# 64-row products of two heads issued alternately into two PSUM banks, and the projections cut into eighths and paced by TensorE time

## The chip, the cores and the metric

One core of one Trainium2 chip runs the program. The time is the device time of that core in microseconds (us). The engines are named as the profile names them: PE is TensorE (PEld its weight loads), DVE is VectorE, ACT is ScalarE, POOL is GpSimd, SP issues the DMAs.

## What is computed

The reference is a trunk of two layers for 1024 latent tokens and 128 context tokens, 1024 wide. Layer 0 (a pooling mixer beside a linear recurrence, then an MLP) is not touched here. In layer 1 one input projection feeds two mixers: a bidirectional RWKV-7 scan with 8 heads of 64, and a bidirectional mLSTM with 4 heads of 128. Their outputs go through one output projection, and an MLP follows.

```python
def step(S, inp):                        # RWKV-7, for each token
    r_t, w_t, k_t, v_t, kk_t, a_t = inp
    sa = jnp.einsum('bhvk,bhk->bhv', S, -kk_t)
    S = (S * w_t[:, :, None, :] + sa[..., None] * (kk_t * a_t)[:, :, None, :]
         + v_t[..., None] * k_t[:, :, None, :])
    y = jnp.einsum('bhvk,bhk->bhv', S, r_t)
    return S, y
...
def odd_mixer(h, P, j, S0, C0, n0, m0):
    z = h @ P['od_w_in'][j]
    zr, zm = jnp.split(z, [RW_COLS], axis=-1)
    y_r, S = rwkv7_mixer(zr, P, j, S0)
    y_m, (C, n, m) = mlstm_mixer(zm, P, j, C0, n0, m0)
    y = jnp.concatenate([y_r, y_m], axis=-1).astype(h.dtype) @ P['od_w_out'][j]
    return y, (S, C, n, m)
```

## The kernel before

The 1152 tokens lie in three blocks of 384 columns (tb). A weight of the large products is split into a high and a low part, so that one 128x128 piece of weight takes three TensorE instructions of 384 columns (L234, L235, L236, function `gemm`). A tile of the input projection (`project`) is 3 blocks of 8 pieces, 24 instructions each.

The change lies in `odd_layer_mixer`, the mixers of layer 1. The RWKV scan is cut into 36 steps: 4 pairs of heads by 9 blocks of 128 tokens. Each block holds four chunks of 64 tokens (u = 0..3, two for each direction), and the two heads of a pair (hh = 0, 1) lie in partitions 0 to 63 and 64 to 127 (`HR`). A step has two parts:

- `prep(n, p, i)`, which does not depend on the scan: loads, the products of the 64-token chunks (tile GB, L1163, 64 rows deep, four for each head), a triangular inverse in fp16 (L1198), and at its end the effect of a chunk on the state (tile EF, L1272, again 64 rows deep, four for each head). For each head the four products fill one PSUM bank, DVE reads it (L1167 and L1168, or L1273), and the next head uses the bank of the same tag again. Two preps are under way at a time, with bank sm0 or sm1 each (`bank = n % 2`).
- `chain_block(p, i)`, the scan itself: two sub-blocks q, the second of which needs the state that DVE makes from the first (L1308). q = 0 uses bank sm2, q = 1 bank sm3. The outputs are read by ACT (L1319) or DVE (L1321).

Beside the scan the main loop of `odd_layer_mixer` emits work from the list `fills`: first `input_pieces`, the rest of the input projection with what follows each tile (`expand`, `gate_part`), and after that `mlstm`. All of these are Python generators: each `yield` ends a piece, and the loop takes pieces from them in turn. In each turn of the loop the chain goes two pieces on, each active prep one, and `fill()` is called 0.29 times (input pieces) or 1.45 times (mLSTM) on average (`R1`, `R2`). A piece of projection is one whole block, 24 TensorE instructions (`GS = 1`). When the list is empty, nothing else is emitted beside the scan.

What the loop emits is the priority, not yet the order: a scheduler orders the instructions of each engine when the program is built. The engines then run their own instructions in that order, and semaphores join them. An fp32 product is one instruction of the program and two records of the trace (so 288 products at L1163 stand as 576); fp16 products and the 384-column ones of `gemm` are one record each.

Of the kernel before, what the change touches and what calls it, by code (L numbers as in the profile page):

```python
# [22 lines left out]
P = 128  # L23
# [25 lines left out]
    pass  # L49

PARAMS = [
    ("c", 8), ("c_ctx", 8), ("norm1_w", 16), ("norm2_w", 16), ("final_norm_w", 8), ("b_mod", 96), ("pool_scale", 4),
# [9 lines left out]
def trunk_kernel(ctx: ExitStack, tc: tile.TileContext, A, outs, dbg=None, upto=99, odd="rm"):  # L64

    nc = tc.nc
# [2 lines left out]
    G.mm, G.wide = 0, True  # L69
    G.split = nc.vector  # L70
    G.odd, G.banks, G.turn = odd, [0, 1, 2, 3], 0
    ve, sc, gp, te, sy = nc.vector, nc.scalar, nc.gpsimd, nc.tensor, nc.sync
# [179 lines left out]
    class Rms:  # L252


        def __init__(self, x):
            self.x, self.acc = x, {}
# [464 lines left out]
    CH = 64  # L721
    DECAY = math.exp(-0.5)
    NCH = NT // P
    HR = [slice(0, 64), slice(64, 128)]
# [3 lines left out]
    def odd_layer_mixer(h, early):  # L728
# [13 lines left out]
        op = es.enter_context(tc.tile_pool(name="op", bufs=1))  # L742
# [6 lines left out]
        Rw = rwkv(zd, zbg, zar, zbk, wend, y, op, fp)  # L749
# [7 lines left out]
        def input_pieces():  # L757
            tiles = [St.tile_g()]
            ml = [St.proj_ml(i) for i in range(16)]
            for p in (1, 2, 3):  # L760
                tiles += [St.proj_rw(p, i) for i in (1, 2, 0)]
                if p == 2:
                    tiles += [St.gates(), -1]
                tiles += [p] + ml[:NML]
                ml = ml[NML:]
            tiles += ml
            side = [(0, St.expand(0))]
            for t in tiles:
                if isinstance(t, int):
                    side.append((t, St.expand(t) if t >= 0 else gate_part()))  # L770
                    continue
                for _ in t:
                    yield
                    if side and not advance(side[0][1]):
# [12 lines left out]
        steps = [(p, i) for p in range(4) for i in range(NCH)]  # L787
# [2 lines left out]
        done = [False] * len(steps)  # L790
        started = [-1, False]

        def fill():

            while fills:
                try:
                    next(fills[0])
                    return
                except StopIteration:
                    fills.pop(0)  # L800
                    if not started[1] and not fills:
                        started[1] = True
                        s1.close()
                        fills.append(mlstm(zm, gates.R, yh, es))

        def advance(g, n=1):
            for _ in range(n):
                try:
                    next(g)
                except StopIteration:  # L810
                    return False
            return True

        while started[0] < 0:
            fill()
        active = {0: preps[0]}
        half = 0
        nstep = len(steps)
        chain, nchain, ready, nxt = None, 0, set(), 1
        quota, urgent = 0.0, []  # L820
        STAG = 11
        R1, R2 = 0.29, 1.45
        while nchain < nstep:
            if chain is None and nchain in ready:
                chain = Rw.chain_block(*steps[nchain])
            if chain is not None and not advance(chain, 2):
                chain = None
                if steps[nchain][1] >= NCH // 2:
                    urgent.append(Rw.finish(*steps[nchain]))
                nchain += 1  # L830
            for n in sorted(active):
                if not advance(active[n]):
                    del active[n]
                    ready.add(n)
            half += 1
            if nxt < nstep and len(active) < 2 and nxt - nchain < NB and (not active or half >= STAG):
                while started[0] < steps[nxt][0]:
                    fill()
                active[nxt] = preps[nxt]
                nxt += 1  # L840
                half = 0
            if urgent and not advance(urgent[0]):
                urgent.pop(0)
            quota += R2 if started[1] else R1
            while quota >= 1.0:
                fill()
                quota -= 1.0
        while fills or urgent:
            if urgent and not advance(urgent[0]):
                urgent.pop(0)  # L850
# [225 lines left out]
    def rwkv(zd, zbg, zar, zbk, wend, y, mp, fp):  # L1076
# [58 lines left out]
        def prep(n, p, i):  # L1135
# [20 lines left out]
            yield  # L1156

            GB = mp.tile([P, 4, 3, CH], F32, tag="GB", name="GB", bufs=2)
            for hh, hr in enumerate(HR):
                pg = smps(bank)  # L1160
                right = cols(AG, hh, PRODUCTS)
                for u in range(4):
                    te.matmul(pg[:, u * P : u * P + P], BK[hr, u], right[hr, u], start=True, stop=True)  # L1163
                pgv = pg.rearrange("p (d c n) -> p d c n", d=2, c=2)
# [103 lines left out]
            for hh, hr in enumerate(HR):  # L1268
                pf = smps(bank)
                right = cols(GB, hh, EFFECT)  # L1270
                for u in range(4):
# [12 lines left out]
        def chain_block(p, i):  # L1284
# [82 lines left out]
        return R_  # L1367

    NB = 3
    GS = 1  # L1370

    class HeadNorm:

# [545 lines left out]
```

## Time and profile before

| | |
|---|---|
| median of 3 runs | 3546.11 us (3545.06 to 3550.35) |
| the profiled execution | 3545.23 us, span of the trace 3543.4 us |
| busy over the span | PE 93%, DVE 57%, ACT 39%, POOL 24% |
| mean granted TensorE clock | 0.947 of 2.4 GHz |
| first products of the scan's step 1 | 1377 us |
| last products of the scan | 2600 us |
| mLSTM, first and last products | 2317 to 2521 us |

The clock column of the profile is the mean of two levels: 1.0 is 2.4 GHz, 0.5 is 1.2 GHz. A mean of 0.95 over a stretch therefore says that a tenth of it ran at the lower one. A busy TensorE counts a product until its result is out; products that follow one another overlap in it.

### The profile page before, as it was taken

Reading aid. Unit: us, or ns where it says so; the run is one execution under the profiler, and the core shown is the slowest. Engines: PE = TensorE matmul, PEld = TensorE weight load, DVE = VectorE, ACT = ScalarE, POOL = GpSimd, SP = SyncE. Lnnn points to the kernel's source line nnn. Section 1 sums busy time; section 2 is a strip of 40 time slices with the busy share of each in tenths; the row PEclk is TensorE's granted clock in tenths of the full one; section 3 lists DMA queues with packets and bytes.
Section 4 is the critical chain, followed back from the end, with each engine's and each line's share of the span. In section 5 each row is a group of like instructions: output and inputs, shape, how many; then the busy total and the mean of one; then the engine's idle time right before and its main releaser. Section 6 shows DMA issues by size and latency. Waiting matters only on the chain. (4 is left out here: it accounts for less than half of the span.)

```text
span 3543.4 us, 54607 instructions
## 1 busy us (share of the span) xinstructions
PE 3312.5 (93%) x21376; PEld 3034.2 (86%) x21376; DVE 2002.5 (57%) x4070; ACT 1385.9 (39%) x2919; POOL 847.5 (24%) x706
## 2 busy tenths in 40 slices
PE   7877999999999987999989899988889999999998
PEld 4766999999999985777777688887679999999998
DVE  6786665555533375677777865567546333333335
ACT  4534332111122254655645565587435122221112
POOL 2232321111111233141232421133013111111112
PEclk9998999999999998988989899999579999999999
DMA  5334312222211124342243422365241111111111
GB/s 207 104 128 159 133 59 85 96 90 90 78 42 42 64 93 123 106 109 80 79 106 97 112 73 71 92 189 150 69 132 64 48 42 42 42 42 42 42 42 72
DMA packets 239971, 313.15 MB, mean 88 GB/s; under 512 B 57362, under 2 KB 183394, under 8 KB 238178
## 3 DMA queue, kind: packets, MB, share of 16 engines
q1 hardware_dynamic: 239714, 309.67, 28.2%
q8 instruction: 168, 2.75, 0.3%
q14 instruction: 89, 0.73, 0.1%
HBM read 250.85 MB, written 58.74 MB: 87 GB/s over the span
## 5 line engine op out<-in xcount | busy, mean ns | idle before, releaser
L234 PE MATMUL mm<-h,w 128*128 128x384 f32 x2552 | 897.6, 352 | 2.3 <-ACT h L503 1.2
L235 PE MATMUL mm<-h,w 128*128 128x384 f32 x2552 | 893.4, 350 | 3.6 <-DVE h L506 1.4
L236 PE MATMUL mm<-h,w 128*128 128x384 f32 x2552 | 891.1, 349 | 2.0 <-POOL w L217 2.0
L217 POOL TENSOR_TENSOR w<-w 128x1024 fp32r<-128x1024 f32 x153 | 371.9, 2431 | 1458.1 <-ACT w L216 1453.6
L216 ACT CAST w<-w 128x1024 fp32r<-128x1024 f32 x211 | 221.1, 1049 | 901.1 <-PE mm L235 779.6
L354 DVE SCALAR_TENSOR_TENSOR x<-mm,mod,x 128x384 f32<-128x384 f32 (+1 forms) x576 | 282.7, 513 | 446.1 <-PE mm L236 419.0
L234 PE MATMUL mm<-uH,w 128*128 128x384 f32 x1536 | 520.0, 339 | 0.0
L236 PE MATMUL mm<-uH,w 128*128 128x384 f32 x1536 | 518.7, 338 | 0.0
L235 PE MATMUL mm<-uL,w 128*128 128x384 f32 x1536 | 518.7, 338 | 0.0
L234 PEld LDWEIGHTS mm<-h,w 128*128 128x128 f32 x2552 | 490.5, 192 | 22.3 <-issue 12.3
L235 PEld LDWEIGHTS mm<-h,w 128*128 128x128 f32 x2552 | 490.9, 192 | 14.8 <-POOL h L506 4.3
L236 PEld LDWEIGHTS mm<-h,w 128*128 128x128 f32 x2552 | 490.7, 192 | 12.2 <-issue 5.3
L374 DVE SCALAR_TENSOR_TENSOR s<-mm,r 128x384 f32<-128x384 f32 x192 | 106.6, 556 | 406.2 <-ACT r L372 406.0
L234 PEld LDWEIGHTS mm<-uH,w 128*128 128x128 f32 x1536 | 288.5, 188 | 2.5 <-issue 2.5
L235 PEld LDWEIGHTS mm<-uL,w 128*128 128x128 f32 x1536 | 288.5, 188 | 0.0
L236 PEld LDWEIGHTS mm<-uH,w 128*128 128x128 f32 x1536 | 288.4, 188 | 0.0
L1111 ACT COPY DB<-YQ 64x256 f16<-64x256 f16 x360 | 144.9, 402 | 152.3 <-DVE YQ L1220 120.0
L372 ACT ACTIVATE r<-mm 128x384 f32<-128x384 f32 x192 | 93.5, 488 | 277.4 <-PE mm L236 276.7
L217 DVE TENSOR_TENSOR uL<-s,uH 128x384 fp32r<-128x384 f32 x192 | 150.2, 782 | 87.6 <-ACT uH L216 87.2
L1220 DVE CAST_PREDICATED YQ<-lm,sm 128x512 f16<-128x512 uint16 x180 | 123.6, 686 | 104.4 <-PE sm L1198 70.4
L1198 PEld LDWEIGHTS <-DB 128*128 128x128 f16 x1728 | 93.6, 104 | 90.0 <-issue 50.3
L216 ACT CAST uH<-s 128x384 fp32r<-128x384 f32 x192 | 98.5, 513 | 143.2 <-DVE s L374 143.1
(374 smaller groups left out, 5121.9 us busy)
## 6 DMA issues: line engine op xcount, KB each, us to landing
w<-in_mlp_w_dram SPq DMA_DIRECT2D x128, 512.0 KB, 3.4
wmod<-in_w_mod_dram SPq DMA_DIRECT2D x80, 512.0 KB, 3.8
w<-in_od_w_in_dram SPq DMA_DIRECT2D x31, 512.0 KB, 3.7
w<-in_od_w_out_dram SPq DMA_DIRECT2D x24, 512.0 KB, 4.0
AG<-zar SPq DMA_DIRECT2D x144, 64.0 KB, 2.3
BK<-zbk SPq DMA_DIRECT2D x72, 128.0 KB, 2.3
hbig<-zm SPq DMA_DIRECT2D x18, 512.0 KB, 4.1
rb<-rowd SPq DMA_DIRECT2D x36, 256.0 KB, 3.7
```

The lines of the kernel that those rows point to most:

```text
L216: sc.copy(Hout, src)
L217: eng.tensor_tensor(Lout, src, Hout.bitcast(F32), op=OP.subtract)
L234: te.matmul(ps, wH[:, k, cols], aH, start=start and k == 0, stop=False)
L235: te.matmul(ps, wH[:, k, cols], aL, start=False, stop=False)
L236: te.matmul(ps, wL[:, k, cols], aH, start=False, stop=stop and k == nk - 1)
L354: ve.scalar_tensor_tensor(xs, ps[:, o], modcol(l, 2 if which == 1 else 5, m, s), xs, op0=OP.mult, op1=OP.add)
L372: sc.activation(r, ps[:, :TB], AF.Relu)
L374: ve.scalar_tensor_tensor(s, ps[:, :TB], 0.0, r, op0=OP.max, op1=OP.mult)
L1111: sc.copy(dst[hr, :, hr], src(hr))
L1198: te.matmul(o[r_, u], lt[r_, u], rt[r_] if rt is i16 else rt[r_, u], start=True, stop=True)
L1220: ve.copy_predicated(YQ.rearrange("p w (d c) n -> p (w d) c n", d=2), lmask(l, 0, 4), pyq.rearrange("p (w c) n -> p w c n", c=2),)
```

## The change

Four things change, all in layer 1's mixers or in how they are emitted.

- `prep`: at both places with 64-row products, the loop over heads and chunks is turned around, so that chunk 0 of head 0 is followed by chunk 0 of head 1 and so on. Head 0 writes the prep's own bank, head 1 bank sm3. DVE reads head 1's bank first. The number of products is the same.
- `chain_block`: both sub-blocks q now write halves of one bank, sm2.
- A projection is emitted in eighths (`GS = 8`): one piece of weight, three TensorE instructions, for each `yield`; `expand` still goes on once for eight of these.
- The loop no longer counts calls of `fill()`. TensorE instructions go through `Counted`, which adds up an assumed time for each (0.175 for a 384-column product of `gemm`, 0.213 for a 128-column fp32 product). `topup(us)` raises a debt and calls `fill()` until the time emitted has reached it: 0.515 in each turn, and half of that after each prep. The chain's two pieces of a turn are put apart, one before the preps and one after.

```diff
+    def matmul(self, out, left, right, **kw):
+        n = math.prod(right.shape[1:])
+        if left.dtype == F16:
+            self.us += max(0.028, n / 2400)
+        elif left.dtype == F32R:
+            self.us += n / 2400 + 0.015
+        else:
+            self.us += 2 * max(n, left.shape[-1] / 1.0) / 1200
+        return self.eng.matmul(out, left, right, **kw)
...
+        def topup(us):
+
+            given[1] += us
+            while fills and given[0] < given[1]:
+                fill()
...
-            if chain is not None and not advance(chain, 2):
+            if chain is not None and not advance(chain, 1):
...
+            topup(DUE)
             for n in sorted(active):
                 if not advance(active[n]):
                     del active[n]
                     ready.add(n)
+                topup(DUE / 2 if active else 0)
...
-            quota += R2 if started[1] else R1
-            while quota >= 1.0:
-                fill()
-                quota -= 1.0
...
-            for hh, hr in enumerate(HR):
-                pf = smps(bank)
-                right = cols(GB, hh, EFFECT)
-                for u in range(4):
-                    te.matmul(pf[:, u * P : u * P + P], WT[hr, u], right[hr, u], start=True, stop=True)
-                ve.tensor_tensor(B.EF[:, hh], pf.rearrange("p (u n) -> p u n", u=4), cols(AG, hh, EFFECT), op=OP.add)
+            rights = [cols(GB, hh, EFFECT) for hh in range(2)]
+            pfs = [smps(bank), smps(3)]
+            for u in range(4):
+                for hh, hr in enumerate(HR):
+                    te.matmul(pfs[hh][:, u * P : u * P + P], WT[hr, u], rights[hh][hr, u], start=True, stop=True)
+            for hh in (1, 0):
+                pf = pfs[hh].rearrange("p (u n) -> p u n", u=4)
+                ve.tensor_tensor(B.EF[:, hh], pf, cols(AG, hh, EFFECT), op=OP.add)
                 yield
...
+            pcs = smps(2).rearrange("p (q d h v) -> p q d h v", q=2, d=2, h=2)
             for q in range(2):
                 us = (1, 2) if q else (0, 3)
-                pc_ = smps(2 + q)[:, : 4 * CH].rearrange("p (d h v) -> p d h v", d=2, h=2)
+                pc_ = pcs[:, q]
...
-    GS = 1
+    GS = 8
```

The order on TensorE at the end of the scan's last step, before (sm is a PSUM bank with the number of its use, GB, WT and EF are tiles of `prep`, XV the state; both uses at L1272 are of the same bank):

```order
L1263 MATMUL sm_26071<-AT_26062,PD_10442 128x128 x4
L1272 MATMUL sm_26079<-GB_25661,WT_26076 128x128 x4
L1272 MATMUL sm_26085<-GB_25661,WT_26076 128x128 x4
L1296 MATMUL sm_26091<-XV_25632,EF_26078 128x64 x4
L1296 MATMUL sm_26100<-XV_25632,EF_26078 128x64 x4
```

The same place in the changed program, where all products stand at a line of `Counted`:

```order
L66 MATMUL sm_26036<-AT_26027,PD_10442 128x128 x4
L66 MATMUL sm_26044<-GB_25390,WT_26041 128x128
L66 MATMUL sm_26045<-GB_25390,WT_26041 128x128
L66 MATMUL sm_26044<-GB_25390,WT_26041 128x128
L66 MATMUL sm_26045<-GB_25390,WT_26041 128x128
L66 MATMUL sm_26044<-GB_25390,WT_26041 128x128
L66 MATMUL sm_26045<-GB_25390,WT_26041 128x128
L66 MATMUL sm_26044<-GB_25390,WT_26041 128x128
L66 MATMUL sm_26045<-GB_25390,WT_26041 128x128
L66 MATMUL sm_26056<-XV_25341,EF_26043 128x64 x8
```

The two heads alternate one by one, each with its own bank. The next rows are the first products (BK, AG) of a step in the middle of the changed program, where the scheduler has placed two of head 0 ahead of two of head 1, with a product of the chain between them:

```order
L66 MATMUL sm_13892<-AG_10447,BK_13866 128x128 x2
L66 MATMUL sm_13844<-XV_13032,EF_13671 128x64 x4
L66 MATMUL sm_13893<-AG_10447,BK_13866 128x128 x2
L66 MATMUL sm_13892<-AG_10447,BK_13866 128x128
L66 MATMUL sm_13893<-AG_10447,BK_13866 128x128
L66 MATMUL sm_13892<-AG_10447,BK_13866 128x128
L66 MATMUL sm_13893<-AG_10447,BK_13866 128x128
```

Here two pairs alternate out of a possible four. Counted over the whole program, 89 pairs of 144 stand next to each other at the first place and 129 of 144 at the second, 218 together; before, it was 1.

The last rows show TensorE while the scan's last step but one ends, before (`mm<-h,w` would be a projection, `hbig` is a tile of the mLSTM):

```order
L1296 MATMUL sm<-XV,EF 128x64 x4
L1198 LDWEIGHTS DB
L1198 MATMUL sm<-YQ,DB 128x64
L1198 LDWEIGHTS DB
L1198 MATMUL sm<-YQ,DB 128x64
```

and at the same place in the changed program:

```order
L66 MATMUL sm<-XV,EF 128x64 x4
L66 LDWEIGHTS DB
L66 MATMUL sm<-YQ,DB 128x64
L66 LDWEIGHTS DB
L66 MATMUL sm<-YQ,DB 128x64
L66 LDWEIGHTS DB
L66 MATMUL sm<-YQ,DB 128x64
L66 LDWEIGHTS DB
L66 MATMUL sm<-YQ,DB 128x64
L70 MATMUL mm<-ident,hbig 128x128 x6
L66 MATMUL mm<-h,w 128x384
L70 MATMUL mm<-ident,hbig 128x128
```

The mLSTM now reaches to the end of the scan: from its last product to the scan's last product TensorE has 357 products before and 77 in the changed program. It begins in both at the same step, the 30th of 36. The number of places at which TensorE turns to a group of 64-row products of `prep` falls from 205 to 144.

## Rows read from the trace of the kernel before

**Rows 1.** The profile's page: the span, and the granted clock in 40 slices.
```profile
span 3543.4 us, 54607 instructions
...
PEclk9998999999999998988989899999579999999999
```

**Rows 2.** Busy time by stretch, layer 1's mixers: stretch, length, engines, clock, DMA.
```profile
core 0: us, PE busy (x) PEld busy (x) DVE busy (x) ACT busy (x) POOL busy (x), PEclk, DMA share, GB/s
...
1377.00:1637.00 260.00, 223.83 (x1605) 180.15 (x1604) 172.31 (x364) 140.07 (x325) 72.39 (x85) 0.84 0.39 105
1637.00:1979.00 342.00, 317.22 (x2570) 262.01 (x2569) 257.29 (x651) 198.52 (x479) 103.40 (x119) 0.94 0.35 94
1979.00:2304.00 325.00, 309.67 (x2666) 261.25 (x2664) 201.13 (x492) 184.26 (x457) 69.08 (x76) 0.94 0.29 85
2304.00:2460.00 156.00, 136.46 (x1292) 123.86 (x1291) 112.11 (x280) 123.22 (x376) 53.05 (x64) 0.98 0.66 183
2460.00:2613.00 153.00, 125.51 (x862) 102.71 (x863) 91.56 (x316) 75.15 (x199) 21.66 (x33) 0.63 0.25 75
2613.00:2700.00 87.00, 87.00 (x502) 86.88 (x500) 47.17 (x75) 36.60 (x54) 23.55 (x18) 1.00 0.40 135
```

**Rows 3.** The same view for three single steps of the scan.
```profile
2136.00:2161.00 25.00, 24.25 (x222) 20.97 (x222) 14.24 (x22) 13.79 (x35) 3.96 (x3) 1.00 0.21 68
...
2004.00:2027.00 23.00, 17.95 (x138) 14.54 (x139) 17.15 (x32) 13.65 (x34) 7.41 (x9) 0.65 0.41 125
1597.00:1637.00 40.00, 39.55 (x297) 32.50 (x296) 25.45 (x70) 21.24 (x51) 7.90 (x8) 0.70 0.22 71
```

**Rows 4.** Groups by line, 1377 to 2613 us: busy, mean ns, idle before.
```profile
L1163 PE MATMUL sm<-AG,BK 64*128 64x128 f32 x576 | 109.4, 320 | 10.1 <-DMA AG<-zar 7.3 <-issue 1.8 <-DVE AG L1168 1.0
...
L1272 PE MATMUL sm<-GB,WT 64*128 64x128 f32 x576 | 92.1, 302 | 7.6 <-DVE EF L1273 5.3 <-ACT WT L1265 2.2
...
L1168 DVE TENSOR_TENSOR AG<-sm,gm 64x512 f32<-64x512 f32 x72 | 49.6, 688 | 2.1
L1273 DVE TENSOR_TENSOR EF<-sm,AG 128x512 f32<-128x512 f32 x72 | 49.5, 688 | 64.2 <-PE sm L1272 61.2 <-DMA AG<-zar 2.7
```

**Rows 5.** TensorE in order of time, near 1900 us: start, length, operation.
```profile
1899.96 0.48 PE L1163 MATMUL sm<-AG,BK 64*128 64x128 f32 x2
...
1903.06 0.34 PE L235 MATMUL mm<-h,w 128*128 128x384 f32 x1
1903.33 1.16 PE L1163 MATMUL sm<-AG,BK 64*128 64x128 f32 x8
1904.41 0.44 PE L236 MATMUL mm<-h,w 128*128 128x384 f32 x1
1904.69 0.34 PE L234 MATMUL mm<-h,w 128*128 128x384 f32 x1
```

**Rows 6.** TensorE in order of time, two 64-row products of `expand`.
```profile
1915.48 0.91 PE L981 MATMUL ex<-wa,lw 64*128 64x384 f32 x2
...
1918.47 0.59 PE L982 MATMUL ex<-wa,lw 64*128 64x384 f32 x1
1918.48 0.59 PE L981 MATMUL ex<-wa,lw 64*128 64x384 f32 x1
1918.90 0.48 PE L982 MATMUL ex<-wa,lw 64*128 64x384 f32 x1
1918.91 0.48 PE L981 MATMUL ex<-wa,lw 64*128 64x384 f32 x1
```

**Rows 7.** Busy time by stretch, the scan's last three steps.
```profile
2460.00:2509.00 49.00, 42.14 (x342) 35.75 (x342) 37.08 (x138) 31.89 (x92) 12.42 (x19) 0.77 0.20 57
2509.00:2544.00 35.00, 32.39 (x181) 24.88 (x179) 17.53 (x57) 15.11 (x39) 2.78 (x4) 0.60 0.31 96
2544.00:2600.00 56.00, 43.55 (x318) 35.32 (x318) 29.55 (x97) 23.36 (x61) 5.55 (x8) 0.56 0.16 51
```

**Rows 8.** TensorE at the end of the last step.
```profile
2590.35 2.07 PE L1272 MATMUL sm<-GB,WT 64*128 64x128 f32 x8 [0.68 <-ACT WT L1265]
2593.21 2.07 PE L1272 MATMUL sm<-GB,WT 64*128 64x128 f32 x8 [0.79 <-DVE EF L1273]
```

**Rows 9.** The readers of the chain's outputs: count, shortest, median and longest ns.
```profile
L1319 ACT COPY ys<-sm x72: 258/260/262, 1458.7 to 2598.6; 64x128 f32<-64x128 f32 x72
...
L1321 DVE TENSOR_TENSOR ys<-ys,sm x72: 272/282/292, 1588.9 to 2600.8; 64x128 f32<-64x128 f32 x72
```

More of the change, by code (lines that the diff above doesn't have):

```diff
@@ L49, with __init__, transpose @@
     pass
+class Counted:
+    def __init__(self, eng):
+        self.eng, self.us = eng, 0.0
+    def matmul(self, out, left, right, **kw):
[7 more added lines that the diff above has]
+        return self.eng.matmul(out, left, right, **kw)
+    def transpose(self, *a):
+        self.us += 0.109
+        return self.eng.transpose(*a)
 PARAMS = [
@@ L71, in trunk_kernel @@
     G.odd, G.banks, G.turn = odd, [0, 1, 2, 3], 0
-    ve, sc, gp, te, sy = nc.vector, nc.scalar, nc.gpsimd, nc.tensor, nc.sync
+    ve, sc, gp, te, sy = nc.vector, nc.scalar, nc.gpsimd, Counted(nc.tensor), nc.sync
     cpool = ctx.enter_context(tc.tile_pool(name="cpool", bufs=1))
@@ L767, in input_pieces @@
             side = [(0, St.expand(0))]
+            n = 0
             for t in tiles:
@@ L773, in input_pieces @@
                     yield
-                    if side and not advance(side[0][1]):
+                    n += 1
+                    if side and n % GS == 0 and not advance(side[0][1]):
                         started[0] = max(started[0], side.pop(0)[0])
@@ L791, in odd_layer_mixer @@
         started = [-1, False]
+        given = [0.0, 0.0]
         def fill():
+            us = te.us
             while fills:
@@ L797, in fill @@
                     next(fills[0])
-                    return
+                    break
                 except StopIteration:
@@ L804, in fill @@
                         fills.append(mlstm(zm, gates.R, yh, es))
+            given[0] += te.us - us
+        def topup(us):
+            given[1] += us
+            while fills and given[0] < given[1]:
+                fill()
         def advance(g, n=1):
@@ L815, in odd_layer_mixer @@
             fill()
+        given[1] = given[0]
         active = {0: preps[0]}
@@ L819, in odd_layer_mixer @@
         chain, nchain, ready, nxt = None, 0, set(), 1
-        quota, urgent = 0.0, []
+        urgent = []
         STAG = 11
-        R1, R2 = 0.29, 1.45
+        DUE = 0.515
         while nchain < nstep:
@@ L834, in odd_layer_mixer @@
                     ready.add(n)
+                topup(DUE / 2 if active else 0)
+            if chain is not None and not advance(chain, 1):
+                chain = None
+                if steps[nchain][1] >= NCH // 2:
+                    urgent.append(Rw.finish(*steps[nchain]))
+                nchain += 1
             half += 1
@@ L1158, in prep @@
             GB = mp.tile([P, 4, 3, CH], F32, tag="GB", name="GB", bufs=2)
-            for hh, hr in enumerate(HR):
-                pg = smps(bank)
-                right = cols(AG, hh, PRODUCTS)
-                for u in range(4):
-                    te.matmul(pg[:, u * P : u * P + P], BK[hr, u], right[hr, u], start=True, stop=True)
-                pgv = pg.rearrange("p (d c n) -> p d c n", d=2, c=2)
+            rights = [cols(AG, hh, PRODUCTS) for hh in range(2)]
+            pgs = [smps(bank), smps(3)]
+            for u in range(4):
+                for hh, hr in enumerate(HR):
+                    te.matmul(pgs[hh][:, u * P : u * P + P], BK[hr, u], rights[hh][hr, u], start=True, stop=True)
+            for hh, hr in reversed(list(enumerate(HR))):
+                right = rights[hh]
+                pgv = pgs[hh].rearrange("p (d c n) -> p d c n", d=2, c=2)
                 gmb = gm[:, hh].unsqueeze(2).to_broadcast([P, 2, 2, P])
@@ L1267, in prep @@
             B.EF = mp.tile([P, 2, 4, P], F32, tag="EF", name="EF", bufs=2)
-            for hh, hr in enumerate(HR):
-                pf = smps(bank)
-                right = cols(GB, hh, EFFECT)
-                for u in range(4):
-                    te.matmul(pf[:, u * P : u * P + P], WT[hr, u], right[hr, u], start=True, stop=True)
-                ve.tensor_tensor(B.EF[:, hh], pf.rearrange("p (u n) -> p u n", u=4), cols(AG, hh, EFFECT), op=OP.add)
+            rights = [cols(GB, hh, EFFECT) for hh in range(2)]
+            pfs = [smps(bank), smps(3)]
+            for u in range(4):
+                for hh, hr in enumerate(HR):
+                    te.matmul(pfs[hh][:, u * P : u * P + P], WT[hr, u], rights[hh][hr, u], start=True, stop=True)
+            for hh in (1, 0):
+                pf = pfs[hh].rearrange("p (u n) -> p u n", u=4)
+                ve.tensor_tensor(B.EF[:, hh], pf, cols(AG, hh, EFFECT), op=OP.add)
                 yield
```

## The prediction

> **What bounds the kernel now.** I first read the page [rows 1]. The clock row shows where to look: from slice 5 on it stands at nine tenths or more, until the mixers of layer 1 begin; there it moves up and down, and it falls to 5 tenths near 2500 us. The change touches nothing else, so only the 1223 us from 1377 to 2600 count; before and after them the sum takes no change.
>
> Next, busy time by stretch [rows 2]. TensorE is busy 86% to 95% of each stretch up to 2304 us, DVE 62% to 75%, ACT 54% to 58%. A busy TensorE could still be one that waits for small products to drain, so the reader should look at one quiet step [rows 3]: from 2136 to 2161 us TensorE is busy 24.25 of 25 us, at full clock, while DVE and ACT are busy for 14 us each. Nobody but TensorE fills that step. A step's length follows TensorE's work: the step at 2004 us has no projection beside it and still takes 23 us, because its clock is 0.65. So in this stage a microsecond of TensorE work that is taken out is mostly a microsecond of time, and a microsecond at the lower clock costs half a microsecond of work.
>
> How much time is spent at the lower clock follows from the mean: a stretch at clock c was there for 2(1-c) of its length. For the first three stretches of [rows 2] that is 0.32 x 260 + 0.12 x 342 + 0.12 x 325 = 163 us; for the last three steps [rows 7] 0.46 x 49 + 0.80 x 35 + 0.88 x 56 = 100 us. The last two of these have little but the scan beside them, since the mLSTM's last product is at 2521 us.
>
> **Part 1: the alternating heads.** 288 products of each kind stand as 576 records [rows 4]. A group of two records takes 0.48 us and one of eight 1.16 us [rows 5], so a record costs (1.16 - 0.48) / 6 = 0.113 us and a product 0.227 us. Whether two products in different halves of the array run side by side can be read from `expand`, whose two products have 64 rows each, in different halves, into different banks [rows 6]: L981 alone takes 0.91 us for its two records; a little later L982 and L981 start 0.01 us apart, twice, and both are done at 1919.39, in 0.92 us. Two cost what one cost. So each pair that stands together in the new order saves one product. The order has 218 such pairs of 288 possible: 218 x 0.227 = 49 us. The lower bound is nothing, if TensorE only waits in the time that it gains; the upper one is 59 us, since about a fifth of the stage runs at the lower clock, where eight records take 2.07 us instead of 1.16 [rows 8]. I take three quarters, **37 us**: in the busiest stretch DVE has a quarter of its time left, and some of what is gained will turn into waiting for it.
>
> A second gain comes with it. A change from `gemm` to 64-row products and back costs TensorE time: in [rows 5] the start of L235 is 0.27 us ahead of the group's first record, and after the group L236 is 0.28 us ahead of L234, where an undisturbed run, the last row of [rows 2], has 87 / 502 = 0.173 us. That is 0.10 us each way. The order has 61 fewer such groups, so 61 x 0.20 = **12 us**; it is between 0 and that if the neighbours were of the same kind. I take it whole.
>
> The Trainium skill, page "TensorEngine Tiling (Array Packing)", section Performance Considerations, speaks against this part: tiling speeds up TensorE and not the reading of PSUM, which may then become the limit. By that rule part 1 would give nothing. The trace says how near that is: DVE reads every bank in question in 0.69 us [rows 4], and already waits for TensorE 61.2 us in total at L1273, which speaks for TensorE as the late one. It is the first rival below.
>
> **Part 2: the fill is spread.** The total of the fill's work does not change, only its place. The last three steps get mLSTM products that stood in earlier steps (357 products of TensorE without mLSTM become 77). What they add there they take away from 2304 to 2460, so the work sums to nothing; the gain is the clock. With mLSTM beside it the clock is 0.98, from 2304 to 2460 us [rows 2]; where it runs out it is 0.56 to 0.77 [rows 7]. If all 100 us went back to full rate, 50 us would be won; if nothing changes, 0. The very last step stays alone in its second half, with 77 products and the latency of each (in [rows 8] TensorE waits for DVE and ACT), so I leave 40 us at the lower clock and take 60 us away: **30 us**.
>
> From 1377 to 2304 the new order spreads the projections a little more evenly: in the order before, the step at 2004 us has no projection at all beside it, and in the new one 62 products. That step alone was 16 us at the lower clock [rows 3]. Elsewhere the scheduler had already cut the blocks into runs of three at the median, before and after the change, so `GS = 8` itself moves little. I take 20 us of the 163 away, **10 us** of time. Bounds: nothing, and 82 us if the clock never falls; a loss is a rival.
>
> **Part 3: what is added.** The sub-block q = 1 of the chain now writes the bank that the outputs of q = 0 are read from, so it waits for two more reads, 0.26 us on ACT or 0.28 us on DVE each [rows 9]: 0.55 x 36 = 20 us if TensorE always stands still for it. Queued behind the waiting product on TensorE are the fp16 products of the two preps, and ACT and DVE wait for those. At the lower bound it is nothing, since the state's own multiplication on DVE has to come first anyway. I take **8 us**. Bank sm3 is shared by two preps and both kinds of product; a collision holds TensorE for two reads of 0.69 us [rows 4]. In the order the products of the second prep are placed after such reads, so I put no cost on it, and leave it to the range (72 uses x 1.4 us = 100 us would be its end). The chain's two pieces set apart and `Counted` cost no instruction.
>
> **The sum.** 37 + 12 + 30 + 10 - 8 = 81 us less than the profiled execution's 3545.23 us: **3464 us**. That execution is 0.9 us below the median of the runs, which I leave out.
>
> **The rivals.**
> *The gain of the pairs is not seen*, since DVE's reads set the pace (the Trainium skill's rule above). For it: DVE is busy 75% from 1637 to 1979 us [rows 2]. Against it: the step of [rows 3] with TensorE alone busy. Without the 37 and 12 us the time is 3513 us. The same time would come if the pairs did not overlap for products of 128 columns.
> *The clock does not recover*: the scan's small products keep it low whatever stands beside them. For it: the step from 1597 to 1637 us has TensorE busy 39.55 of 40 us, with projections, and yet a clock of 0.70 [rows 3]. Against it: 0.98 beside the mLSTM. Without the 30 and 10 us: 3504 us.
> *It recovers everywhere*: three quarters of the 163 us go instead of 20. That is 50 us more, 3414 us. For it: an even rate leaves no step bare; against it the same step at 1597.
> *Slower: the clock falls more often.* Pairs take 1.4 us of TensorE work out of each step (49 / 36), and runs of projection are no longer emitted in blocks; a step like that at 1597 us then becomes the rule. From 1377 to 2304 us, 18% of the time is at the lower clock now. If it were 40%, 371 us, it would cost (371 - 163) / 2 = 104 us in place of the 10 us gained: 3464 + 10 + 104 = 3578 us. It decides from the point where the rest of the gain, 71 us, is eaten: 163 + 142 = 305 us, a third of that stretch.
>
> **How the numbers follow.** The forecast's own case, 3435 to 3490 us, has a chance of 0.53; the pairs unseen 0.12, the clock not recovered 0.14, recovered everywhere 0.10, slower 0.11. The range reaches from the case of full recovery to a little beyond the one with the pairs unseen: **3412 to 3530 us**, which leaves out the slower case and the tails. A measurement of this kernel tells no change from one of about 0.2%, 7 us. Faster by more than that: 0.53 + 0.12 + 0.14 + 0.10 less 0.02 for two small gains that both fail, 0.87; within it 0.04; slower 0.09, since a part of the slow case ends inside.
>
> **What the profile after should show.** At the two 64-row places, records in pairs that start 0.01 us apart, and eight pairs in about 1.2 us. The clock from 2460 us to the end of the scan above 0.8 up to the last step. The scan's end, now at 2600 us, near 2520 us. From 1377 to 2304 us a clock of 0.92 to 0.95; if it is under 0.85, the slow rival is on. L1273's successor should show less waiting for TensorE than 61 us; if DVE is busy above 85% in the middle stretch and TensorE's idle time has grown by some 40 us, the first rival is right. The prediction would also be wrong if the output projection after the scan no longer starts at full rate, as the last row of [rows 2] shows it, because the mLSTM now ends just before it.

## The result, and the profile after

| | before | changed |
|---|---|---|
| median | 3548.23 us (3545.06 to 3558.00, 4 runs) | 3463.37 us (3459.86 to 3466.98, 4 runs) |
| ratio | | 0.9756, 95% interval 0.9733 to 0.9780 |
| profiled execution | 3545.23 us | 3459.86 us |
| span, mean clock | 3543.4 us, 0.947 | 3458.1 us, 0.961 |
| the scan's last product | 2600 us | 2516 us |

The change takes about 85 us, and the scan's end has moved by 84 us: all of it lies in the mixers of layer 1, and the 942 us behind the scan (943 before) are as they were. The forecast was 3464 us. That the total fits does not yet say that its terms do; they are taken apart below.

In the page of the changed kernel, the clock row answers to [rows 1]: in the mixers of layer 1 no slice is under 8 tenths now, where two were at 5 and 7. (The 7 in the fourth slice lies in layer 0, which the change does not touch.)

```profile
span 3458.1 us, 54562 instructions
...
PEclk9997999999999999899999989989899999999999
```

Busy time by stretch of the changed kernel answers to [rows 2]. The first two stretches have the same limits as before; the others end where the corresponding work ends now. (Columns as there.)

```profile
core 0: us, PE busy (x) PEld busy (x) DVE busy (x) ACT busy (x) POOL busy (x), PEclk, DMA share, GB/s
...
1377.00:1637.00 260.00, 220.63 (x1767) 178.36 (x1765) 187.80 (x423) 148.76 (x350) 77.20 (x88) 0.91 0.40 110
1637.00:1979.00 342.00, 311.28 (x2697) 251.21 (x2693) 274.64 (x665) 211.86 (x508) 111.50 (x131) 0.96 0.37 99
1979.00:2252.00 273.00, 257.62 (x2438) 213.59 (x2438) 170.84 (x422) 167.06 (x416) 57.97 (x62) 0.95 0.32 96
...
2530.00:2620.00 90.00, 89.22 (x514) 88.78 (x514) 49.30 (x90) 36.69 (x54) 25.31 (x19) 1.00 0.39 134
```

In the same 260 us TensorE starts 1767 records where it started 1605, at a clock of 0.91 in place of 0.84. DVE is busy 80% of the second stretch, under the 85% that the prediction named as a sign of the first rival. After the scan TensorE is at full rate from 2530 us on, as it was from 2613 us before, in both 13 or 14 us after the scan's last product.

The 64-row products themselves and the chain's (tile XV), from 1377 to 2530 us by line, answer to [rows 4]. All products now stand at L66, a line of the counting class; L1315 is what L1273 was.

```profile
L66 PE MATMUL sm<-XV,EF 128*128 128x64 f32 x576 | 86.5, 292 | 8.2 <-DVE EF L1315 5.9 <-ACT ys L1362 1.6 <-DVE ys L1364 0.4
...
L66 PE MATMUL sm<-AG,BK 64*128 64x128 f32 x576 | 72.6, 313 | 4.8 <-DMA AG<-zar 4.8
...
L66 PE MATMUL sm<-GB,WT 64*128 64x128 f32 x576 | 52.2, 296 | 1.6 <-ACT WT L1305 1.0 <-DVE AG L1208 0.4
...
L1315 DVE TENSOR_TENSOR EF<-sm,AG 128x512 f32<-128x512 f32 x72 | 46.9, 685 | 22.0 <-PE sm L66 22.0
```

The same 1152 records keep TensorE busy for 72.6 + 52.2 = 125 us, where they took 202 us in [rows 4]. DVE waits 22.0 us for them at L1315, where it was 61.2 us at L1273. That alone would also fit a reader that has become the late one; what speaks against it is TensorE's own waiting. It stands 4.8 us for a DMA at the first place and 1.6 us at the second, and only 0.4 us of this is for a DVE reader (L1208). Before, it stood 5.3 us and 1.0 us for the DVE readers at these places [rows 4].

In order of time, at the last two steps (answers to [rows 5] and [rows 8]):

```profile
2480.50 1.16 PE L66 MATMUL sm<-GB,WT 64*128 64x128 f32 x16
...
2507.74 1.96 PE L66 MATMUL sm<-GB,WT 64*128 64x128 f32 x16 [0.68 <-ACT WT L1305]
2510.47 2.14 PE L66 MATMUL sm<-XV,EF 128*128 128x64 f32 x8 [0.77 <-DVE EF L1315]
2513.91 1.97 PE L66 MATMUL sm<-XV,EF 128*128 128x64 f32 x8 [1.30 <-ACT ys L1362]
```

Sixteen records take 1.16 us at the full clock and 1.96 us at the lower one, what eight took before. The last row shows the price of the chain's shared bank in this step: TensorE stands 1.30 us until ACT has read the outputs of q = 0. At the same place before, it stood 0.38 us for DVE's state (L1308).

The last three steps answer to [rows 7]:

```profile
2375.00:2415.00 40.00, 33.01 (x322) 28.31 (x322) 31.27 (x108) 30.15 (x93) 17.28 (x23) 0.91 0.46 131
2415.00:2452.00 37.00, 31.36 (x286) 27.12 (x288) 31.38 (x106) 26.51 (x78) 11.14 (x16) 0.91 0.44 125
2452.00:2516.00 64.00, 49.15 (x382) 40.68 (x382) 44.33 (x171) 34.01 (x91) 8.39 (x12) 0.72 0.26 82
```

Two of the three are at 0.91; the last one, with its bare end, is at 0.72.

### The profile page after: what moved, and what is told of

Its sections match the earlier page's. It is cut to its first block, busy times and chain, and to the rows that moved or that the text cites. A ratio compares the mean times of both kernels' runs of the same rounds, so it can differ in the third digit from the quotient of the medians.

```text
span 3458.1 us, 54562 instructions
## 1 busy us (share of the span) xinstructions
PE 3214.0 (93%) x21376; PEld 2945.3 (85%) x21376; DVE 1994.1 (58%) x4070; ACT 1384.8 (40%) x2919; POOL 851.4 (25%) x706
## 4 chain that ended last, share of the span: by engine, by line
PE 69%; DVE 15%; ACT 7%; issue 4%; POOL 2%; DMA 1%; SPq 0%; DVEq 0%; POOLq 0%; ACTq 0%
PE mm L66 56%; PE sm L66 9%; PE ex L66 2%; PE sm L70 1%; ACT DB L1149 1%; DVE YQ L1260 1%; ACT XV L1274 1%; DVE AG L1208 1%; DVE GB L1207 1%; ACT h L362 1%; DVE xc L1088 1%; DVE nt L359 0%; DVE YQ L1244 0%; POOL ii L629 0%; DMA AG<-zar 0%
## 5 line engine op out<-in xcount | busy, mean ns | idle before, releaser
L66 PE MATMUL mm<-h,w 128*128 128x384 f32 x8808 | 1717.2, 347 | 13.8 <-DVE h L238 3.4
L66 PEld LDWEIGHTS mm<-h,w 128*128 128x128 f32 x8808 | 1546.7, 190 | 55.1 <-issue 16.9
L66 PE MATMUL mm<-uH,w 128*128 128x384 f32 x3072 | 795.3, 338 | 0.4 <-POOL w L238 0.4
L66 PEld LDWEIGHTS mm<-uH,w 128*128 128x128 f32 x3072 | 558.9, 188 | 3.2 <-issue 2.5
L66 PE MATMUL mm<-uL,w 128*128 128x384 f32 x1536 | 518.8, 338 | 0.0
L66 PEld LDWEIGHTS mm<-uL,w 128*128 128x128 f32 x1536 | 288.4, 188 | 0.0
L66 PEld LDWEIGHTS <-DB 128*128 128x128 f16 x2016 | 106.5, 101 | 132.7 <-issue 90.5
L195 DVE SCALAR_TENSOR_TENSOR modacc<-wmod,csl,modacc 128x512 f32<-128x512 f32 x168 | 134.5, 846 | 5.5 <-DMA wmod<-in_w_mod_dram 5.3
L66 PE MATMUL sm<-YQ,DB 128*128 128x64 f16 x1152 | 80.7, 199 | 42.3 <-ACT XV L1274 17.8
L1279 POOL TENSOR_TENSOR DB<-GB,DB 64x256 f16<-64x256 f32 x72 | 50.7, 704 | 262.6 <-PE sm L66 181.8
L238 DVE TENSOR_TENSOR w<-w 128x1024 fp32r<-128x1024 f32 x58 | 76.6, 1327 | 66.7 <-ACT w L237 61.3
L287 POOL TENSOR_TENSOR nacc<-nacc,nsq 128x384 f32<-128x384 f32 x56 | 68.0, 1222 | 140.7 <-ACT nsq L286 109.7
L66 PE MATMUL sm<-XV,EF 128*128 128x64 f32 x576 | 86.5, 292 | 8.2 <-DVE EF L1315 5.9
```

What stands on the lines that cost most here:

```text
L66: return self.eng.matmul(out, left, right, **kw)
L195: ve.scalar_tensor_tensor(acc[:, s], wm[:, i], c, acc[:, s], op0=OP.mult, op1=OP.add)
L238: eng.tensor_tensor(Lout, src, Hout.bitcast(F32), op=OP.subtract)
L287: (eng or (ve if tb == NTB - 1 else gp)).tensor_add(self.acc[tb], self.acc[tb], sq)
L1279: gp.tensor_tensor(N2[hr, :, hr], lower[hh][hr], N1[hr, :, hr], op=OP.subtract)
```

## The experiments

All ratios are against the kernel before on the same chip, with the 95% interval. The stage is split for all of them at the first product of the scan's 30th step: the 29 steps ahead of it run beside projections (where the fill is faster, beside mLSTM too), the seven behind it beside mLSTM or nothing. Time at the lower clock is 2(1 - c) of a stretch's length, from the clock column; its two digits leave about 9 us either way in a stretch of 900. Each stretch is of one execution. The kernel late_spread below does the same work in the first 29 steps as the kernel before, and the two differ there by 6 us of time and 20 us at the lower clock, so differences of that size say nothing. For the kernel before and for the changed one these two stretches are:

```profile
1377.00:2304.00 927.00, 850.72 (x6835) 703.40 (x6834) 630.74 (x1506) 522.86 (x1259) 244.88 (x279) 0.91 0.34 94
2304.00:2600.00 296.00, 254.55 (x2126) 219.82 (x2124) 196.26 (x570) 193.58 (x567) 73.81 (x94) 0.82 0.45 127
```

```profile
1377.00:2250.00 873.00, 787.53 (x6874) 641.34 (x6872) 632.45 (x1507) 526.31 (x1266) 246.67 (x281) 0.94 0.36 101
2250.00:2516.00 266.00, 223.29 (x2082) 194.21 (x2078) 190.59 (x571) 187.76 (x557) 71.00 (x92) 0.87 0.47 135
```

So the change took 54 us in the first part and 30 us in the second.

### Each half of the change alone

**pairs_only** is the kernel before with these edits, and the same at the first place with 64-row products; `R1`, `R2` and `GS = 1` stay.

```diff
+            rights = [cols(GB, hh, EFFECT) for hh in range(2)]
+            pfs = [smps(bank), smps(3)]
+            for u in range(4):
+                for hh, hr in enumerate(HR):
+                    te.matmul(pfs[hh][:, u * P : u * P + P], WT[hr, u], rights[hh][hr, u], start=True, stop=True)
...
+            pcs = smps(2).rearrange("p (q d h v) -> p q d h v", q=2, d=2, h=2)
```

> The kernel before with the alternating heads (and the chain's shared bank), but with the old pacing: whole blocks, 0.29 and 1.45 calls. Its order has 217 pairs of 288. Theory (TensorE bounds the stage, a pair costs one product): 37 + 12 - 8 = 41 us less than before, about 3507 us. Rival (DVE's reads of the banks bound, pairs unseen): within 10 us of before. Rival (all of the gain is the pairs, the clock following from them): 75 us or more less.

Measured: 3486.14 us, ratio 0.9828 (0.9813 to 0.9844), 61 us less. Its two stretches:

```profile
1378.00:2249.00 871.00, 786.02 (x6826) 644.82 (x6824) 624.00 (x1504) 517.51 (x1252) 244.57 (x279) 0.93 0.36 100
2249.00:2540.00 291.00, 246.31 (x2134) 214.54 (x2134) 191.74 (x572) 196.01 (x574) 75.32 (x95) 0.79 0.45 130
```

The first 29 steps take 871 us, as in the full change; the last seven 291 us, nearly as before. The pairs, with the chain's shared bank and without the new pacing, explain the first part of the change, and give more than the theory's 41 us. The last rival, with 75 us or more, is not reached, but part of it is true: the clock of the first 29 steps rises with the pairs, from 0.91 to 0.93.

**pace_only** is the changed kernel with the two places of `prep` and the chain's banks as they were before.

```diff
-            rights = [cols(GB, hh, EFFECT) for hh in range(2)]
-            pfs = [smps(bank), smps(3)]
...
-            pcs = smps(2).rearrange("p (q d h v) -> p q d h v", q=2, d=2, h=2)
+                pc_ = smps(2 + q)[:, : 4 * CH].rearrange("p (d h v) -> p d h v", d=2, h=2)
```

> The changed kernel without the alternation and without the shared bank of the chain: products head by head in one bank, with the new pacing and the eighths. Theory (the fill's place acts through the clock): 40 us less than before, 3508 us, with the lower clock's time falling from 270 us to about 190 us. Rival (the pacing does nothing without the pairs): within 10 us of before.

Measured: 3516.15 us, ratio 0.9907 (0.9891 to 0.9922), 33 us less.

```profile
1378.00:2299.00 921.00, 849.05 (x6873) 697.53 (x6872) 622.84 (x1508) 526.11 (x1266) 248.01 (x281) 0.92 0.35 96
2299.00:2565.00 266.00, 229.94 (x2081) 202.40 (x2077) 191.47 (x567) 187.30 (x555) 71.40 (x92) 0.89 0.48 136
```

The mirror image: 6 us in the first part, 30 us in the second. **late_spread** does the second part with one number in the kernel before:

```diff
-        R1, R2 = 0.29, 1.45
+        R1, R2 = 0.29, 0.90
```

> The kernel before with one number changed: 0.90 calls of the mLSTM per turn in place of 1.45, so that 51 products of TensorE follow the last mLSTM product instead of 357. Theory of the prediction: 30 us less than before (60 of 100 us leave the lower clock in the last three steps). Rival (the late part gives little; the evening out of the projections from 1377 to 2304 us gives most): 15 us less or under.

Measured: 3521.35 us, ratio 0.9922 (0.9907 to 0.9937), 28 us less.

```profile
1379.00:2312.00 933.00, 855.47 (x6833) 706.10 (x6833) 629.91 (x1504) 522.83 (x1257) 245.17 (x279) 0.90 0.34 93
2312.00:2580.00 268.00, 233.81 (x2125) 201.95 (x2125) 191.42 (x570) 192.73 (x568) 74.28 (x94) 0.90 0.49 137
```

It has the last seven steps at 268 us and the first part no shorter than before. So of the 33 us of the new pacing 28 are the later end of the mLSTM, and the evening out of the projections is worth some 5 us, which the intervals do not tell from nothing. The two halves sum to 61 + 33 = 94 us, the change to 0.0244 x 3548 = 87 us; the difference is inside the intervals.

### Is it the alternation or the second bank?

**by_head** keeps the two banks and everything else of the changed kernel, and turns the loops back:

```diff
-            for u in range(4):
-                for hh, hr in enumerate(HR):
+            for hh, hr in enumerate(HR):
+                for u in range(4):
```

> The changed kernel with the two banks kept, but the four products of head 0 emitted ahead of the four of head 1. 66 of 288 pairs still stand together in its order, where the changed kernel has 218. Theory (the products run side by side): 152 x 0.227 = 35 us of TensorE work come back, 26 to 35 us slower than the changed kernel. Rival (what helps is that head 1 need not wait until DVE has read head 0's bank): the same time as the changed kernel within 5 us.

Measured: 3490.30 us, ratio 0.9842 (0.9822 to 0.9862): 27 us slower than the changed kernel by the medians, 30 us by the ratios. This is the size of the 152 lost pairs, 26 to 35 us. Its 64-row records and its two stretches:

```profile
L66 PE MATMUL sm<-AG,BK 64*128 64x128 f32 x576 | 82.5, 312 | 3.8 <-DMA AG<-zar 3.4 <-DMA BK<-zbk 0.3
L66 PE MATMUL sm<-GB,WT 64*128 64x128 f32 x576 | 73.8, 301 | 6.1 <-ACT WT L1305 6.0
```

```profile
1378.00:2288.00 910.00, 828.70 (x6876) 681.54 (x6874) 634.41 (x1506) 526.34 (x1267) 246.29 (x280) 0.91 0.35 96
2288.00:2553.00 265.00, 224.29 (x2080) 195.37 (x2077) 191.51 (x572) 187.89 (x557) 71.53 (x92) 0.90 0.47 137
```

The same 1152 records keep TensorE busy for 156 us in place of 125. The first 29 steps take 910 us in place of 873, at a clock of 0.91 in place of 0.94, so a part of the 27 to 30 us can be the clock: by the mean clocks of all executions, 307 us of the whole span are at the lower one, 286 in the changed kernel, 21 us more, and a half of that is 10 us. The rival is out: with two banks and without the alternation most of the first part's gain is gone. Against pace_only the kernel is 26 us faster; 66 pairs that still stand together would be worth 15 us of this, and no run says what the rest is.

### Doubling the products

**twice_single** doubles each 64-row product in the kernel before, **twice_pairs** each pair in the changed one.

```diff
                 for u in range(4):
-                    te.matmul(pf[:, u * P : u * P + P], WT[hr, u], right[hr, u], start=True, stop=True)
+                    for _ in range(2):
+                        te.matmul(pf[:, u * P : u * P + P], WT[hr, u], right[hr, u], start=True, stop=True)
```

```diff
-            for u in range(4):
+            for u in (0, 0, 1, 1, 2, 2, 3, 3):
                 for hh, hr in enumerate(HR):
```

> The kernel before with each 64-row product of prep issued twice in a row (the second writes the same values again): 576 products more, none of them side by side. Theory (TensorE bounds the stage, 0.227 us a product): 576 x 0.227 = 131 us more than before, somewhat less where TensorE waits, 105 to 131. Rival (DVE's reads bound it, products are covered): under 40 us more.

> The changed kernel with each pair of products issued twice: 576 products more, 513 pairs of 576 stand together in its order, so 639 places of a product in place of 358. Theory: 281 x 0.227 = 64 us more than the changed kernel, 50 to 70. If pairs ran one after the other: 131 us more. If products are covered anyway: under 20 us more.

Measured: twice_single 3636.53 us, ratio 1.0254 (1.0227 to 1.0280), 90 us more than before, where 105 to 131 were expected. twice_pairs 3536.50 us, ratio 0.9966 (0.9949 to 0.9983), 75 us more than the changed kernel by the ratios, where 50 to 70 were expected. Both are far from "covered", so TensorE's work does set the time; but a single product came out too cheap and a pair too dear. The 64-row records over the whole scan, first of twice_single, then of twice_pairs:

```profile
L1164 PE MATMUL sm<-AG,BK 64*128 64x128 f32 x1152 | 182.8, 302 | 14.1 <-issue 6.8 <-DMA AG<-zar 6.5 <-PE sm L1298 0.8
...
L1274 PE MATMUL sm<-GB,WT 64*128 64x128 f32 x1152 | 161.1, 293 | 7.3 <-DVE EF L1275 5.8 <-ACT WT L1266 1.5
```

```profile
L66 PE MATMUL sm<-AG,BK 64*128 64x128 f32 x1150 | 106.5, 307 | 3.1 <-DMA AG<-zar 3.1
...
L66 PE MATMUL sm<-GB,WT 64*128 64x128 f32 x1152 | 89.5, 295 | 3.5 <-ACT WT L1305 3.5
```

As many added products keep TensorE busy for 142 us more when they stand singly (344 for 202) and for 71 us more in pairs (196 for 125). The two stretches of each say what became of this:

```profile
1373.00:2360.00 987.00, 919.24 (x7724) 779.02 (x7724) 632.58 (x1503) 521.53 (x1251) 242.46 (x279) 0.96 0.32 88
2360.00:2690.00 330.00, 299.35 (x2391) 262.83 (x2390) 195.14 (x576) 194.97 (x573) 76.64 (x96) 0.79 0.41 116
```

```profile
1378.00:2320.00 942.00, 853.73 (x7790) 710.01 (x7788) 635.62 (x1507) 524.53 (x1268) 244.31 (x281) 0.91 0.34 94
2320.00:2591.00 271.00, 234.53 (x2315) 204.73 (x2311) 193.06 (x569) 185.92 (x554) 71.59 (x92) 0.88 0.45 131
```

In twice_single TensorE is busy 113 us more and idle 19 us less than before (1219 of 1317 us, where it was 1105 of 1223): 142 us of the doubled records, less 29 us that the other products took less. In twice_pairs it is busy 77 us more and idle 3 us less than in the changed kernel: 71 us of the records and 6 us of the others. The clock goes the same way. In the first 29 steps of twice_single the time at the lower clock falls from 0.18 x 927 = 167 us to 0.08 x 987 = 79 us; in twice_pairs it rises from 0.12 x 873 = 105 us to 0.18 x 942 = 170 us. By the mean clocks of all executions, over the whole span, it falls from 387 to 331 us in the one and rises from 286 to 317 us in the other, which is less. So the clock is a part of why, and less idle time another.

What a microsecond at the lower clock costs can be read between executions of one kernel, where the work is the same: over 117 executions on record here, each compared with the others of its kernel on its chip, the span grows by 0.34 us for each further microsecond at the lower clock. The half that the prediction took is high for this; where a gain of the clock is given below, it is a half, or a range from 0.34 to a half.

### The chain's bank, the eighths, and the whole order of a place

**shared_bank** is the kernel before with only the chain's edit; **whole_blocks** is the changed kernel with `GS = 1`.

```diff
+            pcs = smps(2).rearrange("p (q d h v) -> p q d h v", q=2, d=2, h=2)
...
-                pc_ = smps(2 + q)[:, : 4 * CH].rearrange("p (d h v) -> p d h v", d=2, h=2)
+                pc_ = pcs[:, q]
```

> The kernel before with one edit: both sub-blocks of the chain write halves of bank sm2. Theory of the prediction: 8 us more than before, 0 to 20. Rival (the scheduler puts other work in the wait): within 4 us of before.

> The changed kernel with GS = 1: projections emitted as whole blocks of 24 TensorE instructions, still paced by TensorE time. Theory (the scheduler cuts the blocks anyway): within 8 us of the changed kernel. Rival (the eighths keep the clock up): 20 us more or over.

Measured: shared_bank 3554.18 us, ratio 1.0019 (1.0003 to 1.0034), 7 us more by the ratios (1 to 12), 4 us by the medians. The prediction's 8 us fit, and so does the rival's "within 4 us". TensorE's waits for the readers of the chain's outputs, from 1377 to 2620 us, are small (who waits, for whom, total, times, longest):

```profile
PE sm L1297 <- ACT ys L1320: 1.9, 2, 1.3
...
PE sm L1297 <- DVE ys L1322: 0.8, 2, 0.6
```

The other run, whole_blocks, took 3459.79 us, ratio 0.9759 (0.9734 to 0.9784): the same as the changed kernel, so the eighths by themselves do nothing that these runs can tell.

**atomic** asks the scheduler to keep the eight products of a place together:

```diff
+            with tc.tile_critical():
-            for u in range(4):
-                for hh, hr in enumerate(HR):
-                    te.matmul(pfs[hh][:, u * P : u * P + P], WT[hr, u], rights[hh][hr, u], start=True, stop=True)
+                for u in range(4):
+                    for hh, hr in enumerate(HR):
+                        te.matmul(pfs[hh][:, u * P : u * P + P], WT[hr, u], rights[hh][hr, u], start=True, stop=True)
```

> The changed kernel with the eight products of each place kept in one piece by the scheduler: all 288 pairs stand together in the order (218 in the changed kernel), and the places where TensorE turns to them fall from 144 to 72. Theory (stage = TensorE's work + half of the lower clock's time + a constant): 70 x 0.227 = 16 us of work less and up to 72 x 0.2 = 14 us of turning, 12 to 30 us faster than the changed kernel. Rival (the piece now waits until both banks and all of its inputs are there, and TensorE stands still for it): no gain or slower.

Measured: 3665.48 us, ratio 1.0333 (1.0313 to 1.0353), some 200 us slower than the changed kernel. All 288 pairs run side by side, and the waits around the sections cost many times the 16 us that the 70 pairs more can give. In the waits of 1377 to 2700 us:

```profile
PEld sm L66 <- issue: 171.5, 80, 6.4
...
DVE EF L1317 <- PEq L1311: 115.2, 32, 6.8
...
DVE GB L1208 <- PEq L1199: 97.1, 34, 5.9
```

The last two rows wait for TensorE's sequencer at the section's own lines, which appear in no other kernel here. This run says what such a section costs, and not what full pairing would bring.

### Where the fill ends

Three runs move the end of the fill against the end of the scan. **due_0.60** and **due_0.50** change one number, **warm_last** adds products that nobody reads:

```diff
-        DUE = 0.515
+        DUE = 0.60
```

```diff
-        DUE = 0.515
+        DUE = 0.50
```

```diff
+            while not fills and given[0] < given[1]:
+                spare = exps()
+                for q in range(4):
+                    te.matmul(spare[:, q * P : q * P + P], ident, ident, start=True, stop=True)
+                given[0] += 4 * 0.213
```

> The changed kernel with DUE = 0.60 in place of 0.515: the fill runs faster, the mLSTM begins at step 25 in place of 30 and 788 products of TensorE follow its last one (77 in the changed kernel, 357 before). Theory (the bare end costs clock): more than the kernel before lost there, 40 to 60 us slower than the changed kernel. Rival (the end does not matter, only the pairs do): within 10 us.

> The changed kernel with DUE = 0.50: the last mLSTM product comes just after the scan's last product. Theory: the last step has cover to its end, 0 to 10 us faster; rival: the mLSTM's end holds up the output projection, 5 to 15 us slower.

> The changed kernel with TensorE products of the identity by itself, which nobody reads, emitted at the same rate once the list of fills is empty: 37 products in the scan's last step. Theory (what the last step loses is the clock): 10 of its 35 us at the lower clock go, about as much as the 37 products add (37 x 0.227 = 8 us): within 5 us of the changed kernel. Rival (low clock is all): 10 us faster or more.

Measured: due_0.60 3501.08 us, ratio 0.9873 (0.9851 to 0.9894), 38 us slower than the changed kernel by the medians and 42 us by the ratios, at the low end of the 40 to 60 expected. due_0.50 3445.95 us, ratio 0.9715 (0.9695 to 0.9735), 17 us faster by the medians and 15 us by the ratios; its slowest execution (3449.22) is faster than the fastest of the changed kernel (3459.86). It is the fastest kernel here, better than the 0 to 10 us of its theory, and its rival, which had it slower, is out. warm_last 3457.31 us, ratio 0.9756 (0.9734 to 0.9778), the same as the changed kernel.

The last seven steps of due_0.60 and of due_0.50:

```profile
2328.00:2569.00 241.00, 191.25 (x1566) 157.27 (x1565) 149.45 (x435) 129.17 (x359) 34.33 (x49) 0.64 0.22 65
```

```profile
2235.00:2494.00 259.00, 218.98 (x2108) 190.62 (x2106) 185.97 (x557) 188.22 (x555) 77.35 (x96) 0.90 0.50 141
```

With the fill gone early, 1566 records take 241 us at a clock of 0.64; with the fill up to the end, 2108 take 259 us at 0.90. In due_0.50 the first 29 steps begin 4 us later and are 19 us shorter (1381 to 2235 us), the last seven are 7 us shorter, and what follows the scan is 952 us in place of 942. The 19 us are not all gain: the first part has 6815 records in place of 6874, so some of its work has moved behind it. The rival was right in this, that what follows the scan grows, by 10 us against 26; just after the scan TensorE stands 3.0 us for a tile of the mLSTM (hbig). In warm_last the last seven steps go from 266 to 260 us, which its profile shows and its median cannot tell from nothing.

## Why the prediction was right

**TensorE bounds the stage: shown.** Doubled products cost 90 and 75 us. TensorE's idle time did not grow by the 40 us that the first rival would have shown: 927 - 850.72 = 76 us in the first part before, 873 - 787.53 = 85 us after. It stands 0.4 us for DVE's reads at the second place, and none is listed at the first. So the first rival is out.

**Part 1, the pairs: mechanism right, size too small.** 37 + 12 - 8 = 41 us was the term, with the bank; pairs_only gives 61 us (55 to 66). Sixteen records take the time of eight, and a doubled pair keeps TensorE busy for half as long as two doubled single products. In the two stretches of pairs_only TensorE is busy 73 us less than before (1032 for 1105) and idle 12 us more (130 for 118). The prediction had 49 + 12 = 61 us of work and 12 + 8 = 20 us of waiting: too little of the one and too much of the other. The missing work fits the clock, which the prediction had put under the new pacing alone: by the mean clocks of all executions the time at the lower clock falls from 381 to 343 us, and 38 us of it are worth 13 to 19 us. No run holds the clock still, so this stays a reckoning, and no run separates the 12 us of the changes of kind from the pairs.

**Part 2, late: size right.** 30 us predicted; 28 us by one number in the kernel before, and 30 us in the last seven steps of the change. Dose and sign follow the end of the fill from due_0.60 to due_0.50. Where the 30 us come from was only half right: the clock of the last seven steps rises from 0.82 to 0.87, which is 107 us at the lower clock becoming 69 us and gives 19 us at most. In the last three steps alone 100 us become 50, where the prediction left 40, and the four steps ahead of them lose a little. In late_spread the 107 us become 54 us, and give up to 26 of 28. In the change the rest would go to the pairs' work in these steps; that is argued, not measured.

**Part 2, the middle: not seen.** 10 us for an even rate of projections; pace_only gives 6 us in the first part, late_spread, which leaves this part as it was, minus 6, and whole_blocks says that the eighths do nothing that can be told. The step at 2004 us of [rows 3] has projections beside it in the new order, and this was worth little over the whole part. The reading of that step was also too simple: TensorE was idle for 5 of its 23 us, so its length was not the clock alone.

**Part 3, the bank: not contradicted.** 8 us predicted, 7 us measured (1 to 12). TensorE's waits for the two readers sum to 2.7 us in shared_bank and to 2.0 us in the changed kernel, far under the 20 us of the upper bound.

**Sum.** 41 + 30 + 10 = 81 us predicted; 61 + 28 + about 5 measured one by one, 85 to 87 together. That 81 lies so near to 85 is partly luck: the pairs were put 20 us too low, against this stand the middle term, which the runs do not tell from nothing, and the 7 to 9 us by which the parts measured one by one exceed the whole, which is within their intervals. The clock as a whole was sized well. By the mean clocks of all executions, 286 us are at the lower one in the changed kernel and 379 to 387 before; some 97 us less are worth 33 to 49 us, where the two clock terms had 40. But about four tenths of this came with the pairs and not with the pacing. The slower rival did not come: less TensorE work in each step went with less time at the lower clock, not more.

## What to carry to other kernels

In this kernel two products of 64 rows, in opposite halves of the array and in different PSUM banks, cost TensorE the time of one where nothing stood between them (sixteen records in 1.16 us, as eight before); no run tried both in one bank. Count in the built order how many pairs stay together and not in the source: 218 against 66 of them made 27 to 30 us here. Where a chain of small products runs beside work that can be placed freely, let that work end with the chain and not ahead of it: one number (`R2`) was worth 28 us here, and another (`DUE`) 15 to 17 us more when the changed kernel was tuned to the end. Buying the last pairs with a section that the scheduler may not cut cost some 200 us, for pairs worth 16.

## What was not expected

The granted clock answered against the direction that I would have guessed, and not in one direction. Pairs took work off TensorE and the time at the lower clock in the first 29 steps fell from 167 to 105 us; doubling single products raised the work and it fell to 79 us; doubling the pairs raised the work and it rose to 170 us, about the value before. By the mean clocks of all executions, over the whole span, the signs are the same and the steps smaller: 379 to 387 us before, 286 in the changed kernel, 331 in twice_single, 317 in twice_pairs. The share of that part in which TensorE is busy does not order them: 0.92 (before), 0.90 (after), 0.93 (twice_single), 0.91 (twice_pairs). What decides between the two levels in this mix of products stays open.
